# Token loads, attention bias rows, the gate store's queue and the place of four inverses, changed together in a two-layer hybrid backbone

## The chip, the cores and the metric

The kernel runs on one core of a Trainium2 chip. The metric is the device time of one execution in microseconds; where several runs were made, it is their median. The profile comes from one further execution.

## What is computed

A backbone of two layers over 256 latent tokens of 2048 features, with 256 context tokens. Layer 0 runs eight heads of a chunked, bidirectional gated DeltaNet beside eight heads of 2-D neighbourhood attention, all from one input projection; layer 1 is a gated short convolution. Each layer also has a SwiGLU feed-forward part of 5632 hidden features, and every normalised input is shifted and scaled by a modulation vector that is itself a product with a weight matrix. Cut to what matters here:

```python
sh1, sc1, g1, sh2, sc2, g2 = jnp.split(jax.nn.silu(c) @ ada_w[l] + ada_b[l], 6, axis=-1)
h = rmsnorm(x_lat, norm_mix[l]) * (1 + sc1) + sh1            # the same for the context tokens, with c_ctx
# gated DeltaNet: per 64-token chunk a triangular inverse, then a scan over the chunks
t_inv = lax.linalg.triangular_solve(eye + m, eye, left_side=True, lower=True, unit_diagonal=True)
# neighbourhood attention: bias by relative position, inside a band of columns only
s_loc = jnp.einsum('brqhd,brjkhd->bhrqjk', qg, kg) * scale + bias[None]
s_loc = jnp.where(in_win[:, None, :], s_loc, -jnp.inf)
# the DeltaNet output is normalised and gated, then both kinds of heads go through one projection
y_gdn = rmsnorm(o, g_norm) * jax.nn.silu(heads(z))
y = jnp.concatenate([y_gdn, y_na], axis=-1) @ w_out
```

## The kernel before

All matrices are float32. Every large product is made as three matmuls: a weight block of 128 x 1024 values is loaded (tile `raw`, L229), ScalarE rounds it to a high part (`whi`, L172), VectorE takes the rest (`wlo`, L243), and TensorE adds high times high, high times low and low times high. `fm_stream` (L306) leaves the result by features, `tm_stream` (L274) by tokens; each step of such a stream is one block of 128 input features. Four `raw` tiles are in flight, so the loads run a few steps ahead of TensorE.

The start. `start_block` (L524) loads 4 MB of the modulation weights in eight pieces (`araw0`, L530) and multiplies them by the conditioning vector (L533); `token_stats` (L565) loads the 512 tokens (`xn`, L569), squares them on ScalarE (L573), and scales them by their inverse norm on VectorE (L576). `start_tokens` (L537) turns one block's product into shift and scale (L540 to L552), transposes the scaled tokens, modulates them on ScalarE (L560, tile `modt`) and casts the result to `h` (L561, L562). The first stream, for the keys, takes up each block of `h` as it comes. Eight such blocks follow one another.

The middle. The projections for the attention queries, keys and values (`QB`, `KB`, `VB`) run as counted steps: 32 for the two halves of the queries, then 16 each for a half of the keys, a half of the values, and the same again. Beside them stands the gated DeltaNet. A list `plan` (L1127) says after which counted step its four pieces are queued, by the numbers in `P_INV`: the first inverse of the context, the second one with the matrices of the latent chunks and the context scans, the first inverse of the latent chunks, and the second one with the latent scores and scans (`first_inverse`, `second_inverse`, `latents`). `inverses` (L939) puts a 64-token inverse together from 32 x 32 blocks: small matmuls (L962, L969, L975), a copy with a minus sign on VectorE (L977) and one on ScalarE (L979). Its blocks come back from a scratch array by sixteen small loads on SyncE (L936). The rest of the modulation, `ada_mixer` (L366), is summed on VectorE (`acc`, L389) from loads on SyncE (`araw`, L384) and closed on TensorE (L396); it runs beside all of this.

The end of the mixer. `na_scores` (L1172) loads one head's bias rows in two halves into `br`, adds the band mask on VectorE into `bq` (L1183), makes the scores (L1187, L1188) and the softmax; `na_values` (L1200) makes the outputs. `za_evac` (L1215) makes the DeltaNet's gate with Silu from the last projection and stores it to the scratch array `zd`; `latent_out` reads it back after the scans. Then the output projection (`ev_w_out`) runs as a stream, in the order of the input groups 2, 0, 1, 3: two groups of attention heads around the two of DeltaNet heads.

Each engine works through its own queue in order, and so do the queues of the DMA issues. A scheduler at build time sets the order within each queue from a model of the engines, so an edit also moves instructions that it doesn't name. SyncE issues nearly all loads and stores; a wait in its queue holds back everything behind it.

Of the kernel before, what the change touches and what calls it, by code (L numbers as in the profile page):

```python
# [23 lines left out]
F32 = mybir.dt.float32  # L24
F32R = mybir.dt.float32r
AF = mybir.ActivationFunctionType
OP = mybir.AluOpType
# [12 lines left out]
GH = 6  # L40
YO = (2, 0, 1, 3)
NPT = 1
P_INV = (30, 32, 79, 80)
AB = 6
AHEAD = 6
LAG = 3
# [62 lines left out]
def body(tc, x, c, ctx, c_ctx, ada_w, ada_b, norm_mix, norm_ffn, ffn_w_gate, ffn_w_up, ffn_w_down,  # L109
# [3 lines left out]
    PE, ACT, DVE, POOL, SP = nc.tensor, nc.scalar, nc.vector, nc.gpsimd, nc.sync  # L113
# [410 lines left out]
    def start_block(b):  # L524

        pr = smt()
        for g in range(0, KT, 4):
            raw = sp.tile([128, 4, 2, 256], F32, name="araw0", tag="araw0", bufs=4)
            for s in range(2):
                SP.dma_start(raw[:, :, s, :], adr[:, g:g + 4, s, b * 256:(b + 1) * 256])  # L530
            for j in range(4):

                PE.matmul(pr[32 * j:32 * j + 32, :], cT2[:, g + j, :], raw[:, j].rearrange("p s n -> p (s n)"),  # L533
                          start=g == 0, stop=g == KT - 4)
        return pr
# [62 lines left out]
    zd = dram.tile([128, 2, 1024], F32, name="zd")  # L598
# [96 lines left out]
    def qa_evac(q):  # L695
# [11 lines left out]
                SP.dma_start(qTd[:, q * 4 + g * 2:q * 4 + g * 2 + 2, :], qf)  # L707
        return head_evac(2, q, 16, done, True)

    sums = start_block(0)  # L710
    token_stats()
    ka = [ka_evac(q) for q in range(2)]
    s0 = fm_stream([(wv, C_KA, 512)], ks, [0, 1], ka[0])
    s1 = fm_stream([(wv, C_KA + 512, 256)], ks, [0, 1], ka[1], gdt)
# [37 lines left out]
    for w in range(2):  # L752
        o = pw[:, w * 256:(w + 1) * 256]
# [407 lines left out]
    nap = pool("na", stack=nastk)  # L1161
# [3 lines left out]
    bandf = C("band")  # L1165
# [6 lines left out]
    def na_scores(h):  # L1172
        kb = nap.tile([128, 512], F32, name="kb", tag="kb", bufs=2)
        qb = nap.tile([128, 256], F32, name="qb", tag="qb", bufs=2)
        bq = nap.tile([128, 6, 64], F32, name="bq", tag="bq", bufs=2)
        br = nap.tile([128, 6, 64], F32, name="br", tag="br", bufs=1)
        for half in range(2):
            src = bass.AP(tensor=ev_rpb.tensor, offset=ev_rpb.offset + h * 465 + (5 - half) * 31 + 15 - 63,
                          ap=[[1, 64], [31, 6], [1, 64]])
            SP.dma_start(br[half * 64:half * 64 + 64], src)  # L1180
        SP.dma_start(kb, kb_d[:, h, :])
        SP.dma_start(qb, qb_d[:, h, :])
        DVE.tensor_tensor(bq, br, bandf[:, None, :].to_broadcast([128, 6, 64]), op=OP.add)  # L1183
        out_ = []
        for t in range(2):
            p = nat(h)
            PE.matmul(p, qb[:, t * 128:(t + 1) * 128], kb, start=True, stop=False)  # L1187
            PE.matmul(p[:, 0:256], C("flip"), bq[:, 2 - 2 * t:6 - 2 * t, :].rearrange("p s c -> p (s c)"),  # L1188
                      start=False, stop=True)
            s = nap.tile([128, 512], F32, name="s", tag="s", bufs=4)  # L1190
            m = nap.tile([128, 1], F32, name="m", tag="m", bufs=4)
            DVE.tensor_reduce(m, p, axis=AX.X, op=OP.max, negate=True)
            l = nap.tile([128, 1], F32, name="l", tag="l", bufs=4)
            ACT.activation(s, p, AF.Exp, bias=m, accum_out=l)
            DVE.reciprocal(l, l)
            DVE.tensor_scalar(s, s, l, None, op0=OP.mult)
            out_.append(s)
        return out_
# [16 lines left out]
    def za_evac(ti, n, p):  # L1215
        o = nsp.tile([128, 512], F32, name="zst", tag="nst", bufs=NST)
        ACT.activation(o, p, AF.Silu)
        ov = o.rearrange("p (h e) -> p h e", h=4)
        DVE.tensor_tensor(ov, ov, gnb[:, None, :].to_broadcast([128, 4, 128]), op=OP.mult)
        SP.dma_start(zd[:, ti, n * 512:(n + 1) * 512], o)  # L1220

    held = na_scores(0)
    for h in range(8):
# [279 lines left out]
```

## Time and profile before

| | |
|---|---|
| median of 3 runs | 2819.64 us (2818.58 to 2827.38) |
| the profiled execution | 2823.79 us |
| its span | 2822.0 us |
| mean granted TensorE clock | 0.989 |
| busy: TensorE, VectorE, ScalarE, GpSimd | 2719.8, 1920.1, 1301.9, 50.3 us |
| moved by DMA | 680.78 MB |

A row of the timeline has the start in us, the length in us, the engine, the line in the code, the operation, out<-in and how many instructions were merged; in brackets stands the idle time of the engine just before it and what ended it. SPq is SyncE's queue of DMA issues: its length is the issue, not the transfer. PE is TensorE, ACT ScalarE, DVE VectorE, POOL GpSimd. A row of the windows has the stretch, its length, and for each engine the busy time with the number of instructions, then the granted clock of TensorE, the share of time in which the DMA engines were busy, and GB/s.

### The profile page before, as it was taken

How to read it: one execution, taken by the hardware profiler on the slowest of the kernel's cores; microseconds unless marked ns; L12 is line 12 of the kernel's file. 1: busy time of each engine (PE TensorE's matmuls, PEld its weight loads, DVE VectorE, ACT ScalarE, POOL GpSimd, SP SyncE). 2: the span in 40 equal slices, each digit the busy share in tenths (PEclk: the TensorE clock that was granted, in tenths of full speed). 3: DMA queues.
4: the chain of work that ended last, by engine and by line, in shares of the span. 5: the costliest groups of instructions: out<-in, count | busy, mean ns of one | idle time of the engine just before them, and what ended most of it. 6: DMA issues, size and time to landing. Idle time of an engine off the chain costs nothing.

```text
span 2822.0 us, 40405 instructions
## 1 busy us (share of the span) xinstructions
PE 2719.8 (96%) x15113; PEld 2277.5 (81%) x15113; DVE 1920.1 (68%) x2647; ACT 1301.9 (46%) x1943; POOL 50.3 (2%) x77
## 2 busy tenths in 40 slices
PE   5999989999999999999999999999999999999998
PEld 3799989887778788888888878878878888888886
DVE  2377768866767888776678667797678644445665
ACT  2267534322454544444455555444454444444554
POOL 0000100000000000000000000000000000000000
PEclk9999999999999999999999999999999999999999
DMA  9945578887758699987788647998559766656663
GB/s 342 325 135 157 148 234 259 270 250 226 213 200 285 208 333 340 345 291 255 264 283 286 197 154 275 333 327 286 186 196 326 247 193 186 187 188 215 190 192 126
DMA packets 286399, 680.78 MB, mean 241 GB/s; under 512 B 57209, under 2 KB 100833, under 8 KB 284795
## 3 DMA queue, kind: packets, MB, share of 16 engines
q1 hardware_dynamic: 281828, 668.73, 71.3%
q10 hardware_dynamic: 4375, 9.48, 0.9%
q8 instruction: 118, 1.93, 0.3%
q14 instruction: 78, 0.64, 0.1%
HBM read 657.63 MB, written 20.48 MB: 240 GB/s over the span
## 4 chain that ended last, share of the span: by engine, by line
PE 78%; DMA 10%; DVE 6%; ACT 3%; issue 2%; SPq 1%; DVEq 0%; POOL 0%; ACTq 0%
PE mm L294 19%; PE mm L291 19%; PE mm L292 19%; PE mm L321 7%; DMA araw<-in_ada_w_dram 5%; PE mm L300 2%; PE mm L301 2%; PE mm L302 2%; DVE wlo L243 2%; PE sm L191 2%; DMA raw<-in_od_w_in_dram 1%; PE sm L533 1%; DVE acc L346 1%; DVE acc L389 1%; PE gd L321 1%
## 5 line engine op out<-in xcount | busy, mean ns | idle before, releaser
L243 DVE TENSOR_TENSOR wlo<-raw,whi 128x1024 fp32r<-128x1024 f32 x800 | 971.1, 1222 | 436.8 <-ACT whi L172 430.9
L172 ACT ACTIVATE whi<-raw 128x1024 fp32r<-128x1024 f32 x800 | 842.2, 1059 | 825.6 <-PE mm L294 618.9
L292 PE MATMUL mm<-wlo,fhi 128*128 128x512 f32 x1232 | 472.4, 392 | 0.0
L291 PE MATMUL mm<-whi,fhi 128*128 128x512 f32 x1232 | 470.7, 396 | 0.0
L294 PE MATMUL mm<-whi,flo 128*128 128x512 f32 x1232 | 392.2, 392 | 0.1
L346 DVE SCALAR_TENSOR_TENSOR acc<-araw,cT,acc 128x1024 f32<-128x1024 f32 x224 | 287.3, 1283 | 130.2 <-DMA araw<-in_ada_w_dram 123.5
L294 PEld LDWEIGHTS mm<-whi,flo 128*128 128x128 f32 x1232 | 230.8, 188 | 51.1 <-DVE flo L1288 0.5
L292 PEld LDWEIGHTS mm<-wlo,fhi 128*128 128x128 f32 x1232 | 231.8, 188 | 48.7
L291 PEld LDWEIGHTS mm<-whi,fhi 128*128 128x128 f32 x1232 | 231.9, 188 | 48.2
L291 PE MATMUL mm<-whi,ahi 128*128 128x512 f32 x672 | 259.8, 392 | 0.0
L292 PE MATMUL mm<-wlo,ahi 128*128 128x512 f32 x672 | 259.3, 391 | 0.0
L294 PE MATMUL mm<-whi,alo 128*128 128x512 f32 x672 | 209.8, 392 | 0.0
L321 PE MATMUL mm<-hllo,whi 128*128 128x256 f32 x608 | 172.9, 289 | 0.0
L321 PE MATMUL mm<-hlhi,whi 128*128 128x256 f32 x570 | 161.7, 292 | 2.2 <-DVE hlhi L561 1.9
L175 ACT ACTIVATE ahi<-prodT 128x256 fp32r<-128x256 f32 x176 | 73.2, 417 | 194.6 <-PE mm L292 183.9
L389 DVE SCALAR_TENSOR_TENSOR acc<-araw,cT,acc 128x512 f32<-128x512 f32 x192 | 142.7, 747 | 29.1 <-DMA araw<-in_ada_w_dram 27.3
L321 PE MATMUL mm<-hlhi,wlo 128*128 128x256 f32 x570 | 157.8, 289 | 0.0
L292 PEld LDWEIGHTS mm<-wlo,ahi 128*128 128x128 f32 x672 | 126.2, 188 | 27.7
L294 PEld LDWEIGHTS mm<-whi,alo 128*128 128x128 f32 x672 | 126.1, 188 | 27.3
L291 PEld LDWEIGHTS mm<-whi,ahi 128*128 128x128 f32 x672 | 126.2, 188 | 27.1
L292 PE MATMUL mm<-wlo,dhi 128*128 128x512 f32 x336 | 126.4, 396 | 2.2 <-DVE wlo L243 2.2
L291 PE MATMUL mm<-whi,dhi 128*128 128x512 f32 x336 | 123.8, 397 | 0.6 <-DVE u_t L1428 0.6
(419 smaller groups left out, 4194.0 us busy)
## 6 DMA issues: line engine op xcount, KB each, us to landing
araw<-in_ada_w_dram SPq DMA_DIRECT2D x288, 512.0 KB
raw<-in_ffn_w_down_dram SPq DMA_DIRECT2D x176, 512.0 KB
raw<-in_ffn_w_gate_dram SPq DMA_DIRECT2D x160, 512.0 KB
raw<-in_ffn_w_up_dram SPq DMA_DIRECT2D x160, 512.0 KB
raw<-in_ev_w_in_dram SPq DMA_DIRECT2D x112, 512.0 KB
araw<-in_ada_w_dram SPq DMA_DIRECT2D x192, 256.0 KB
raw<-in_od_w_in_dram SPq DMA_DIRECT2D x96, 512.0 KB
raw<-in_ev_w_out_dram SPq DMA_DIRECT2D x32, 512.0 KB
```

Source lines behind the costliest of these rows:

```text
L172: ACT.activation(dst, src, AF.Copy)
L175: ACT.activation(hi, src, AF.Copy)
L191: return PE.transpose(dst, src, ident[:n, :n])
L243: last_lo[0] = DVE.tensor_tensor(lo, raw, hi, op=OP.subtract).ins
L291: PE.matmul(ps[ti][n], a, hi[:, n * 512:(n + 1) * 512], start=first, stop=False)
L292: PE.matmul(ps[ti][n], a, lo[:, n * 512:(n + 1) * 512], start=False, stop=False)
L294: last_mm[0] = PE.matmul(ps[ti][n], b, hi[:, n * 512:(n + 1) * 512], start=False, stop=False).ins
L300: PE.matmul(ps[ti][n], lh(t), hi[:, c_], start=False, stop=False)
L301: PE.matmul(ps[ti][n], lh(t), lo[:, c_], start=False, stop=False)
L321: last_mm[0] = PE.matmul(ps[f][:, n * 256:(n + 1) * 256], wt, mv(w, k), start=False, stop=i == len(ks) - 1 and g == len(group) - 1 and j = ...
L346: DVE.scalar_tensor_tensor(acc, raw, cT[:, k:k + 1], acc, op0=OP.mult, op1=OP.add)
L389: DVE.scalar_tensor_tensor(accs[n], raws.pop(i), cT[:, k:k + 1], accs[n], op0=OP.mult, op1=OP.add)
```

## The change

There are four edits. The tokens' loads and statistics come ahead of the first block of modulation weights. The bias rows are loaded straight into `bq`, which gets a third buffer, and the mask is added in place; the tile `br` is gone. The gate's store to `zd` is issued by GpSimd instead of SyncE. The four pieces of the DeltaNet are queued two counted steps later each.

```diff
--- before.py
+++ after.py
@@ -40,7 +40,7 @@
 GH = 6
 YO = (2, 0, 1, 3)
 NPT = 1
-P_INV = (30, 32, 79, 80)
+P_INV = (32, 34, 81, 82)
 AB = 6
 AHEAD = 6
 LAG = 3
@@ -707,8 +707,8 @@
                 SP.dma_start(qTd[:, q * 4 + g * 2:q * 4 + g * 2 + 2, :], qf)
         return head_evac(2, q, 16, done, True)
 
+    token_stats()
     sums = start_block(0)
-    token_stats()
     ka = [ka_evac(q) for q in range(2)]
     s0 = fm_stream([(wv, C_KA, 512)], ks, [0, 1], ka[0])
     s1 = fm_stream([(wv, C_KA + 512, 256)], ks, [0, 1], ka[1], gdt)
@@ -1172,15 +1172,14 @@
     def na_scores(h):
         kb = nap.tile([128, 512], F32, name="kb", tag="kb", bufs=2)
         qb = nap.tile([128, 256], F32, name="qb", tag="qb", bufs=2)
-        bq = nap.tile([128, 6, 64], F32, name="bq", tag="bq", bufs=2)
-        br = nap.tile([128, 6, 64], F32, name="br", tag="br", bufs=1)
+        bq = nap.tile([128, 6, 64], F32, name="bq", tag="bq", bufs=3)
         for half in range(2):
             src = bass.AP(tensor=ev_rpb.tensor, offset=ev_rpb.offset + h * 465 + (5 - half) * 31 + 15 - 63,
                           ap=[[1, 64], [31, 6], [1, 64]])
-            SP.dma_start(br[half * 64:half * 64 + 64], src)
+            SP.dma_start(bq[half * 64:half * 64 + 64], src)
         SP.dma_start(kb, kb_d[:, h, :])
         SP.dma_start(qb, qb_d[:, h, :])
-        DVE.tensor_tensor(bq, br, bandf[:, None, :].to_broadcast([128, 6, 64]), op=OP.add)
+        DVE.tensor_tensor(bq, bq, bandf[:, None, :].to_broadcast([128, 6, 64]), op=OP.add)
         out_ = []
         for t in range(2):
             p = nat(h)
@@ -1217,7 +1216,7 @@
         ACT.activation(o, p, AF.Silu)
         ov = o.rearrange("p (h e) -> p h e", h=4)
         DVE.tensor_tensor(ov, ov, gnb[:, None, :].to_broadcast([128, 4, 128]), op=OP.mult)
-        SP.dma_start(zd[:, ti, n * 512:(n + 1) * 512], o)
+        POOL.dma_start(zd[:, ti, n * 512:(n + 1) * 512], o)
 
     held = na_scores(0)
     for h in range(8):
```

From L1176 on a line's number is one lower in the changed code. What the scheduler makes of the change, at three places. First SyncE at the start of the program; `araw` is a block's modulation weights (two loads a row), `xn` the tokens, `raw` the stream's weights. Before:

```order
L493 DMA cs<-in_cst_dram 128x128
L530 DMA araw_144<-in_ada_w_dram 128x4x256 x2
L530 DMA araw_151<-in_ada_w_dram 128x4x256 x2
L530 DMA araw_158<-in_ada_w_dram 128x4x256 x2
L530 DMA araw_165<-in_ada_w_dram 128x4x256 x2
L569 DMA xn<-in_x_dram 128x2048 x2
L569 DMA xn<-in_ctx_dram 128x2048 x2
L530 DMA araw_241<-in_ada_w_dram 128x4x256 x2
L229 DMA raw<-in_ev_w_in_dram 128x2x512
```

and now:

```order
L493 DMA cs<-in_cst_dram 128x128
L569 DMA xn<-in_x_dram 128x2048 x2
L569 DMA xn<-in_ctx_dram 128x2048 x2
L530 DMA araw_176<-in_ada_w_dram 128x4x256 x2
L530 DMA araw_183<-in_ada_w_dram 128x4x256 x2
L530 DMA araw_190<-in_ada_w_dram 128x4x256 x2
L530 DMA araw_197<-in_ada_w_dram 128x4x256 x2
L229 DMA raw<-in_ev_w_in_dram 128x2x512
```

The four loads of tokens moved from behind the first block's eight weight loads to their front, and the first stream weights stand ahead of the second block's loads.

Then TensorE at the first inverse. `hlhi` and `hllo` are the two parts of the latent tokens, `hclo` is the context's, `xd` and `n` are the inverse's blocks, `acc` the mixer's modulation. Before, its small matmuls followed one another, with 24 stream matmuls of the query projection still behind them:

```order
L321 MATMUL mm<-hllo,whi 128x256
L321 MATMUL mm<-hlhi,wlo 128x256
L962 MATMUL gd<-xd,n_3970 32x32 x32
L396 MATMUL sm<-cs,acc 128x1 x4
L969 MATMUL gd<-xdT,Y 32x32 x32
L975 MATMUL gd<-Y,xdT 32x32 x32
L321 MATMUL mm<-hlhi,whi 128x256
L321 MATMUL mm<-hllo,whi 128x256
```

Now the inverse begins after those 24, at the boundary to the key projection (L317 is its first matmul, `h_100` the first feature block of the tokens), and the sums of `acc` stand ahead of the 24:

```order
L321 MATMUL mm<-hlhi,wlo 128x256 x2
L321 MATMUL mm<-hlhi,whi 128x256
L321 MATMUL mm<-hllo,whi 128x256
L321 MATMUL mm<-hlhi,wlo 128x256
L962 MATMUL gd<-xd,n_3970 32x32 x32
L317 MATMUL mm<-h_100,whi 128x512
L321 MATMUL mm<-hllo,whi 128x256
L321 MATMUL mm<-hclo,whi 128x256
L321 MATMUL mm<-h_100,wlo 128x256 x2
```

The inverse's second group, L969, now stands behind 22 matmuls of the key projection instead of right behind the first. The third inverse moved in the same way, from 48 matmuls ahead of the boundary between the second keys and the second values to 38 matmuls (of 512 columns) behind it.

Last, SyncE around the first weights of the output projection (`ev_w_out`). Before, the gate's stores (`zd`) stand among them:

```order
L384 DMA araw<-in_ada_w_dram 128x512 x2
L1220 DMA zd<-zst 128x512 x2
L1202 DMA vb<-vb_d 128x4x128
L1220 DMA zd<-zst 128x512
L229 DMA raw<-in_ev_w_out_dram 128x1024 x2
L1181 DMA kb<-kb_d 128x512
L1182 DMA qb<-qb_d 128x256
L229 DMA raw<-in_ev_w_out_dram 128x1024
```

and now:

```order
L384 DMA araw<-in_ada_w_dram 128x512 x2
L229 DMA raw<-in_ev_w_out_dram 128x1024 x6
L1201 DMA vb<-vb_d 128x4x128
L229 DMA raw<-in_ev_w_out_dram 128x1024
L384 DMA araw<-in_ada_w_dram 128x512
L229 DMA raw<-in_ev_w_out_dram 128x1024
```

The stores left for GpSimd's queue; the loads of the attention heads stand elsewhere among the weights. On ScalarE the same stretch, where `zst` is the gate, `s` and `PT` belong to the attention, `yhi` is an output, and `o_t` and `vn` belong to the scans. Before:

```order
L1217 ACT_TABLE_LOAD
L1217 ACTIVATE zst<-mm 128x512 x2
L175 ACTIVATE yhi<-sm 128x256
L1194 ACT_TABLE_LOAD
L1194 ACTIVATE s,l<-sm,m 128x512
L1217 ACT_TABLE_LOAD
L1217 ACTIVATE zst<-mm 128x512
L1038 ACTIVATE vn<-gd,beta 128x128 x4
L1217 ACTIVATE zst<-mm 128x512
```

and now:

```order
L1193 ACTIVATE s,l<-sm,m 128x512
L1216 ACT_TABLE_LOAD
L1216 ACTIVATE zst<-mm 128x512 x4
L1016 ACTIVATE o_t<-gd,eg 128x128 x4
L172 ACTIVATE whi<-raw 128x1024
L175 ACTIVATE yhi<-sm 128x256
L172 ACTIVATE whi<-raw 128x1024
L1024 ACTIVATE vd<-gd,brest 128x128 x4
```

The four gates follow one another, with one load of the Silu table ahead of them instead of two.

## The prediction

> **What bounds the kernel now.** I read the page first (span, busy time, chain), then the windows, then the timeline of each engine at the four places where the code changes.
>
> ```profile
> span 2822.0 us, 40405 instructions
> PE 2719.8 (96%) x15113; PEld 2277.5 (81%) x15113; DVE 1920.1 (68%) x2647; ACT 1301.9 (46%) x1943; POOL 50.3 (2%) x77
> PE 78%; DMA 10%; DVE 6%; ACT 3%; issue 2%; SPq 1%; DVEq 0%; POOL 0%; ACTq 0%
> ```
>
> TensorE is busy for 2719.8 of 2822.0 us, so at most 102 us can be won without taking work away, and the change takes none away: it only moves waits. The order of the instructions is the same from the later part of the output projection on, so the whole effect lies before that. In the next two windows (us; then PE busy, its instructions, the other engines, PEclk, DMA share, GB/s) TensorE is full: 0.114 us for a 256-column matmul of the stream, 0.227 us for a 512-column one.
>
> ```profile
> 580.00:590.00 10.00, 10.00 (x88) 10.00 (x87) 5.75 (x10) 2.57 (x6) 1.81 (x1) 1.00 0.84 172
> 890.00:900.00 10.00, 10.00 (x44) 8.07 (x43) 9.81 (x11) 4.10 (x4) 0.00 (x0) 1.00 0.95 332
> ```
>
> **Part 1, tokens ahead of the modulation weights.** Timeline of the start:
>
> ```profile
> 14.96 0.82 SPq L569 DMA_DIRECT2D xn<-in_x_dram  x2
> 21.26 1.94 PE L533 MATMUL sm<-araw,cT 128*32 128x512 f32 x8 [1.15 <-DMA araw<-in_ada_w_dram]
> 26.17 0.16 DVE L552 TENSOR_TENSOR sc<-sc,vecT 128x4 f32<-128x4 f32 x1
> 30.99 1.91 ACT L573 ACTIVATE junk<-xn 128x2048 f32<-128x2048 f32 x1 [0.51 <-DMA xn<-in_ctx_dram]
> 35.30 1.06 ACT L172 ACTIVATE whi<-raw 128x1024 fp32r<-128x1024 f32 x1 [0.79 <-DMA raw<-in_ev_w_in_dram]
> 35.34 4.87 DVE L576 TENSOR_SCALAR xn<-xn,n0r 128x2048 f32<-128x2048 f32 x4
> 40.78 1.93 ACT L560 ACTIVATE modt<-sm,sh,sc 128x256 f32<-128x256 f32 x4 [1.59 <-PE sm L191]
> 45.43 2.08 PE L317 MATMUL mm<-h,whi 128*128 128x512 f32 x4
> ```
>
> Shift and scale are ready at 26.33, but the last tokens land only at 30.99, and their squares, the root and the four scalings (4.87) then stand bare until the first modulated tile at 40.78; the stream starts at 45.43, 4.65 later. With the tokens first, that statistics work lies beside the weight loads, and the weights land last, at about 31 (the same bytes in the same queue). From the last L533 to a ready scale it is 26.33 - 21.26 = 5.1, so 31 + 5.1 + 4.65 = 40.7 at the latest; the first weight of the stream, too, has the two loads of the next block (1 MB) no longer ahead of it. Gain 4.7, and up to 6.5 if the 8 KB rows of the tokens load faster than the weights' 1 KB rows. Does it survive? The load is near its limit until 140:
>
> ```profile
> 100.00:120.00 20.00, 20.00 (x168) 16.48 (x167) 7.62 (x21) 5.75 (x9) 0.00 (x0) 1.00 1.00 320
> 120.00:140.00 20.00, 20.00 (x168) 14.35 (x166) 8.48 (x20) 5.00 (x9) 0.00 (x0) 1.00 1.05 333
> 140.00:160.00 20.00, 20.00 (x169) 18.58 (x162) 8.43 (x19) 7.33 (x12) 0.00 (x0) 1.00 0.44 144
> 142.34 0.99 PE sm L533 x8
> ```
>
> The DMA share falls only after 140, and the last weights of this stage are used at 142.34. TensorE is full here, so it is the bound, but by little: a TensorE that runs 5 us ahead would want those bytes at 137. I take -4.5, with ends -6.5 and 0. That cover is what the term rests on.
>
> **Part 2, bias rows straight into their tile.** The DMA and the add stay, the intermediate tile with one buffer goes, so head 1's and head 2's rows no longer wait for the add of the head before.
>
> ```profile
> 687.34 1.13 PE L838 MATMUL gd<-cs,gm 128*128 128x128 f32 x8 [0.50 <-DVE gm L834]
> 696.13 0.56 DVE L1183 TENSOR_TENSOR bq<-br,cs 128x384 f32<-128x384 f32 x1 [5.74 <-DMA br<-in_ev_rpb_dram]
> 697.88 0.50 PE L292 MATMUL mm<-wlo,hlhi 128*128 128x512 f32 x1 [2.27 <-DVE wlo L243]
> 701.60 2.08 PE L838 MATMUL gd<-cs,gm 128*128 128x128 f32 x8 [2.99 <-DVE AT L1074]
> 705.93 0.56 DVE L1183 TENSOR_TENSOR bq<-br,cs 128x384 f32<-128x384 f32 x1 [3.79 <-DMA br<-in_ev_rpb_dram]
> 700.00:710.00 10.00, 8.40 (x27) 6.13 (x28) 6.21 (x13) 2.98 (x6) 0.00 (x0) 0.68 0.65 167
> ```
>
> VectorE takes its queue in order: for 5.74 us it waits for the rows, and the weight split and the mask product behind it keep TensorE waiting 2.27 and 2.99. After that TensorE runs at 0.68 of its clock: 8.40 us of work that at full clock is 5.7, so 2.7 more, and the same eight L838 take 2.08 instead of 1.13. Together 8.0. The Trainium skill (TensorE: Matmul & The Clock Gate, Part 1) has the clock fall only after an idle window of about 3.4 us; by that neither wait would slow it and the term would be at most 5.3, but the 0.68 stands in the row, so the trace decides. In the new order head 1's rows are asked for right behind head 0's, yet still on the same busy queue, so some of the wait may stay: I take -5, ends -8 and 0.
>
> **Part 3, gate store from GpSimd.** SyncE's queue and what hangs on it:
>
> ```profile
> 764.05 0.57 SPq L1202 DMA_DIRECT2D vb<-vb_d  x1
> 768.79 0.69 DVE L1219 TENSOR_TENSOR zst<-zst,gnb 128x512 f32<-128x512 f32 x1 [1.22 <-ACT zst L1217]
> 769.51 0.32 SPq L1220 DMA_DIRECT2D zd<-zst  x1
> 769.88 0.92 SPq L229 DMA_DIRECT2D raw<-in_ev_w_out_dram  x2
> 776.41 1.20 PE L291 MATMUL mm<-whi,yhi 128*128 128x512 f32 x4 [3.01 <-ACT whi L172]
> 388.37 7.68 DMA qb_d<-nst
> ```
>
> SyncE stands from 764.6 to 769.5 behind a store whose tile VectorE has not finished, and the first weights of the output projection are issued only then; TensorE waits 3.01 for them. Moved to GpSimd's idle queue the store holds nobody. But the new order of ScalarE puts the four gates one behind the other, and with two tiles the third has to wait until the first store has landed, with VectorE's next scan step behind it. No row shows a store from GpSimd; the nearest is one of the same kind of tile from SyncE, 7.68 us. Covered, the term is -3.0; bare, the wait is 7.68 instead of 3.01, +4.7. I take -1.5, since the loads of the stream, which sat ahead of that store in its own queue, aren't ahead of this one. The Trainium skill's fit for a GpSimd DMA (DMA: Bandwidth & Descriptors, Anatomy of one DMA) would make it 2.6 us, an estimate; by it the term is -3.0.
>
> **Part 4, inverses two steps later.**
>
> ```profile
> 415.20 2.21 SPq L229 DMA_DIRECT2D raw<-in_ev_w_in_dram  x4
> 415.26 0.75 PE L962 MATMUL gd<-xd,n 32*32 32x32 f32 x64
> 415.98 1.02 PE L396 MATMUL sm<-cs,acc 128*128 128x1 f32 x8
> 420.81 1.06 ACT L172 ACTIVATE whi<-raw 128x1024 fp32r<-128x1024 f32 x1 [4.37 <-DMA raw<-in_ev_w_in_dram]
> 421.08 0.48 PE L975 MATMUL gd<-Y,xdT 32*32 32x32 f32 x18 [2.98 <-issue]
> 421.92 0.58 PE L321 MATMUL mm<-hlhi,whi 128*128 128x256 f32 x1 [0.36 <-ACT whi L172]
> 420.00:430.00 10.00, 8.56 (x88) 8.13 (x88) 7.98 (x11) 7.18 (x13) 0.00 (x0) 0.67 0.87 275
> 616.29 0.44 PE L962 MATMUL gd<-xd,n 64*64 64x64 f32 x2 [4.13 <-DVE xd L977]
> ```
>
> The weights that TensorE needs after 415.26 are issued at 415.20, behind the inverse's own loads, and land at 420.81. So the 6.66 us to 421.92 are a wait for weights, of which TensorE uses 6.66 - 2.98 - 0.36 = 3.3, about 0.9 of it for the mixer's sums (L396), which stay where they are, and 2.4 for the first inverse. In the new order the inverse stands behind the two steps that wait for those weights, and its 2.4 us come later: +2.4. The third inverse waited 4.13 for a copy on VectorE; 14.3 us later in the stream (48 matmuls of 0.114 before the boundary of two streams, now 38 of 0.227 behind it, 5.5 + 8.6) the copy should be due in time: -4.1 to 0, I take -2. The latent scans start later, too, and at their end more of them may stand bare. A step there is 4.99 us long:
>
> ```profile
> 810.92 1.06 PE L1000 MATMUL gd<-state,kT 128*128 128x128 f32 x8
> 815.91 1.06 PE L1000 MATMUL gd<-state,kT 128*128 128x128 f32 x8
> ```
>
> TensorE works for most of such a step, so one more costs a part of it: +1.6, ends 0 and 5. Part 4 together: +2, ends -4 and +7.
>
> **The sum.** -4.5 - 5 - 1.5 + 2 = -9.0. The profiled execution took 2823.79 (span 2822.0 and 1.8 around it), 4.2 above the median of 2819.64, so I make the sum against it, 2814.8, and take the same 9.0 off the median: 2810.6, given as 2811.
>
> **The rivals.** *The same bytes on the same engines.* Parts 1 and 3 only reorder transfers. If the loads until 140 are what TensorE really follows, and the output weights land no earlier, both are worth nothing: -5 + 2 = -3, 2817. For it: the DMA shares of 1.00 and 1.05. Against it: TensorE full there, and SyncE's 4.9 us stand. The Trainium skill says the like (DMA: Bandwidth & Descriptors, Issuing engines are not separate DMA queues): another issuer saves only the sequencer's time; that would be the 0.32 us of the store's row, while the trace has the wait. *Every wait goes* (the lower ends): -6.5 - 8 - 3 - 4 = -21.5, 2798. For it: each wait has one releaser which the change moves; against it: some of the covers compete for one DMA queue. *Slower: the latent chain becomes the bound.* From the third inverse to the last scan each step hangs on the one before. If the 14.3 us by which it is queued later aren't made up, group 0 of the output projection comes 14.3 later, and the waits of parts 2 and 3, which lie beside that chain, give nothing: 14.3 - 4.5 = +9.8, 2829. It decides as soon as TensorE has no stream matmul left while scans remain, as between 810.92 and 815.91, where the order has none; against it: a step has four or more groups of eight matmuls like the rows above, so most of its 4.99 us is TensorE's own work, which costs the same wherever it stands. *The change doesn't do what it says*: the rows of the orders show that it does, 0.
>
> **How the numbers follow.** A measurement of this kernel can tell about 0.3%, 8.5 us, from no change: 2811.2 is the line. Forecast 0.45 (2805 to 2817: 0.27 below the line, 0.18 above), same bytes 0.20, every wait goes 0.20, slower 0.15. Faster 0.27 + 0.20 = 0.47, within 0.18 + 0.20 = 0.38, slower 0.15. The range takes in the lower ends at 2798 and leaves out most of the slower case: 2798 to 2826.
>
> **What would show it.** Right: the first L317 near 40 and no new wait for araw before 140; no VectorE wait over 2 us for head 1's and head 2's rows, and a clock of 1.00 where the 0.68 stands; the output weights issued before the last gate. Wrong: TensorE waiting for L533's data between 60 and 140; ScalarE waiting for a GpSimd store; a wait of over 5 us ahead of the first inverse's weights; the last scan more than 10 us behind the last stream matmul of the first half's group 2.

## The result, and the profile after

The changed kernel takes 2837.75 us (median of 6 runs, 2834.55 to 2840.86), the kernel before 2825.08 beside it (6 runs, 2818.58 to 2828.2). The ratio is 1.0048, with a 95% interval of 1.0035 to 1.0060: some 12.7 us slower, where 9 us faster was forecast. The profiled execution of the changed kernel took 2834.55 us, the fastest of its six, with a span of 2832.8, 10.8 more than the one before.

The head of its page:

```profile
span 2832.8 us, 40395 instructions
PE 2726.1 (96%) x15113; PEld 2282.1 (81%) x15113; DVE 1920.6 (68%) x2647; ACT 1297.7 (46%) x1940; POOL 58.2 (2%) x81
```

The number of TensorE's instructions is the same, and its busy time rose by 6.3 us: waiting, and work at a lower clock, not more work. The last transposition of the softmax weights into `sm` (L191) starts at 834.23 before and at 846.42 after, 12.2 later; the two spans differ by 10.8, so nothing is added behind it. The loss is ahead of that point, as the prediction had said that the whole effect would be.

**Start (part 1).** TensorE's timeline: the first matmul of the stream, and the last group of the modulation.

```profile
38.52 2.07 PE L317 MATMUL mm<-h,whi 128*128 128x512 f32 x4 [0.57 <-DVE h L561]
149.61 0.95 PE L546 MATMUL sm<-cs,mrow 128*128 128x2 f32 x8
```

The stream starts 6.9 us earlier (38.52 against 45.43), and the last group of the modulation starts 3.1 later (149.61 against 146.48 before), behind as many matmuls as before (850 and 851). In two windows of that stretch (us; PE busy, then the other engines, PEclk, DMA share, GB/s) TensorE's clock is lower:

```profile
60.00:80.00 20.00, 18.93 (x134) 12.63 (x134) 5.91 (x14) 4.04 (x6) 0.00 (x0) 0.91 1.09 353
100.00:120.00 20.00, 18.50 (x138) 12.94 (x137) 6.51 (x15) 4.04 (x6) 0.00 (x0) 0.91 0.90 291
```

Before, the first of them was no fuller, but at full clock:

```profile
60.00:80.00 20.00, 18.51 (x146) 12.69 (x146) 7.73 (x21) 4.80 (x8) 0.00 (x0) 1.00 1.05 335
```

The second was full and had 168 matmuls in the prediction's row, against 138 here. SyncE's waits between 0 and 160 show who holds the loads: SyncE waits for TensorE to free the buffers of `araw` (us in total, times, longest).

```profile
SPq L530 <- PE sm L533: 30.0, 17, 4.1
```

Before, that was 16.8 us in 12 waits. The modulation matmuls stand in TensorE's order between matmuls of the stream, which now starts sooner.

**Bias rows (part 2).** Two of VectorE's eight bias additions (start, us, engine and line, tile, idle time before and its releaser):

```profile
694.73 0.56 DVE L1182 TENSOR_TENSOR bq<-bq,cs 128x384 f32<-128x384 f32 x1 [1.71 <-DMA bq<-in_ev_rpb_dram]
758.31 0.56 DVE L1182 TENSOR_TENSOR bq<-bq,cs 128x384 f32<-128x384 f32 x1 [4.64 <-DMA bq<-in_ev_rpb_dram]
```

The first of them is head 2's. The 5.74 and 3.79 us of heads 1 and 2 are down to 1.57 and 1.71. But all eight additions now wait for their rows, 19.2 us together, where four waited 14.6. SyncE issues the rows of the later heads about as late as before, and the addition stands sooner behind them: the rows for the addition at 758.31 are issued at 749.87; before, those for the one at 770.45 were issued at 752.39.

**Gate store (part 3).** ScalarE's third Silu; then VectorE's first multiplication, GpSimd's first store, the chain's piece for its transfer, and TensorE behind all that:

```profile
769.93 0.60 ACT L1216 ACTIVATE zst<-mm 128x512 f32<-128x512 f32 x1 [13.12 <-DMA zd<-zst]
```

```profile
759.82 0.68 DVE L1218 TENSOR_TENSOR zst<-zst,gnb 128x512 f32<-128x512 f32 x1
760.81 0.68 POOL L1219 DMA_DIRECT2D zd<-zst  x1 [89.34 <-DVE zst L1218]
760.81 9.01 DMA zd<-zst
772.35 2.08 PE L1020 MATMUL gd<-R,xdT 128*128 128x128 f32 x8 [7.01 <-DVE R L1003]
```

The first gate is through Silu at 754.86. VectorE, in order, waits until 758.31 for bias rows, so it multiplies the gate at 759.82, GpSimd issues the store at 760.81, and it lands 9.01 later. Until then the third Silu has no tile: 13.12 us of ScalarE, and 7.01 of TensorE, since VectorE's `R` stands behind the third gate. This is the bare end of part 3, made longer by part 2.

**Inverses (part 4).** TensorE at the wait for weights near 415, the first inverse, the first scan, the last stream matmul of group 2 and the last scan:

```profile
423.26 0.58 PE L321 MATMUL mm<-hlhi,whi 128*128 128x256 f32 x1 [7.87 <-ACT whi L172]
428.65 0.75 PE L962 MATMUL gd<-xd,n 32*32 32x32 f32 x64
524.48 1.05 PE L1020 MATMUL gd<-vtok,xdT 128*128 128x128 f32 x8
801.07 0.63 PE L294 MATMUL mm<-whi,ylo 128*128 128x512 f32 x2
830.44 1.16 PE L1020 MATMUL gd<-R,xdT 128*128 128x128 f32 x8 [0.24 <-DVE R L1003]
```

The wait is 7.87 us and empty. The scans start 19.3 later than before (505.17) and end 12.2 later (818.26). Between the last stream matmul and the last scan there are 29.4 us, before 20.4.

### The profile page after: what moved, and what is told of

It reads as the page before. It is cut to its first block, busy times and chain, and to the rows that moved or that the text cites. A ratio compares the mean times of both kernels' runs of the same rounds, so it can differ in the third digit from the quotient of the medians.

```text
span 2832.8 us, 40395 instructions
## 1 busy us (share of the span) xinstructions
PE 2726.1 (96%) x15113; PEld 2282.1 (81%) x15113; DVE 1920.6 (68%) x2647; ACT 1297.7 (46%) x1940; POOL 58.2 (2%) x81
## 3 DMA queue, kind: packets, MB, share of 16 engines
q0 software_dynamic: 320, 1.05, 0.1%
## 4 chain that ended last, share of the span: by engine, by line
PE 76%; DMA 11%; DVE 6%; ACT 3%; issue 3%; SPq 1%; DVEq 0%; POOL 0%; ACTq 0%
PE mm L291 17%; PE mm L294 17%; PE mm L292 17%; PE mm L321 10%; DMA araw<-in_ada_w_dram 6%; DVE wlo L243 2%; PE sm L191 2%; DVE acc L346 2%; PE mm L300 2%; PE mm L302 2%; PE mm L301 2%; DMA bq<-in_ev_rpb_dram 1%; PE sm L533 1%; PE gd L321 1%; ACT whi L172 1%
## 5 line engine op out<-in xcount | busy, mean ns | idle before, releaser
L321 PE MATMUL mm<-hlhi,whi 128*128 128x256 f32 x570 | 161.9, 292 | 10.8 <-ACT whi L172 7.9
```

What stands on the lines that cost most here:

```text
L321: last_mm[0] = PE.matmul(ps[f][:, n * 256:(n + 1) * 256], wt, mv(w, k), start=False, stop=i == len(ks) - 1 and g == len(group) - 1 and j = ...
```

## The experiments

Each kernel was timed against the kernel before on the same chip; the ratio is to those runs. In all, 18 further kernels ran. The four entries of `P_INV` are called the first pair (first inverse; second inverse with the scans behind it) and the last pair. My first theory, from the trace above, was **scans late**: the chain from the first inverse to the last scan starts 19 us late and ends the stretch. Its rivals were the gate store and the start.

### One part at a time on the kernel before

Tokens alone:

```diff
-    sums = start_block(0)
     token_stats()
+    sums = start_block(0)
```

> The kernel before with the tokens first and nothing else. Theory scans late (the two inverses, queued two steps later, start the delta-rule scans some 19 us later and these end the stretch): nothing of the loss is here; the kernel stays within 3 us of before, first L317 near 38.5 instead of 45.43, and whatever the start gains or loses is taken up by the time the scans begin. Theory gate store (the third Silu waits for the store that GpSimd issued, and the scans' work behind it on ScalarE is late): the same. Theory start (the transfers, not TensorE, are the bound up to 145 us, and the tokens first leave the DMA engines idle for part of the first 20 us): the last modulation row L546 is 3 us later than before and the kernel 2 to 4 us slower.

Measured: 2828.28 us, ratio 1.0015 (1.0002 to 1.0029). The last group of the modulation:

```profile
150.17 0.95 PE L546 MATMUL sm<-cs,mrow 128*128 128x2 f32 x8
```

The stream starts 6.9 us earlier, at 38.53, and the modulation ends 3.7 later. So part 1 doesn't gain 4.5; it loses about 4.

Bias rows alone:

```diff
-        bq = nap.tile([128, 6, 64], F32, name="bq", tag="bq", bufs=2)
-        br = nap.tile([128, 6, 64], F32, name="br", tag="br", bufs=1)
+        bq = nap.tile([128, 6, 64], F32, name="bq", tag="bq", bufs=3)
...
-        DVE.tensor_tensor(bq, br, bandf[:, None, :].to_broadcast([128, 6, 64]), op=OP.add)
+        DVE.tensor_tensor(bq, bq, bandf[:, None, :].to_broadcast([128, 6, 64]), op=OP.add)
```

> The kernel before with the bias rows straight into their tile. All theories: within 3 us of before. Where the prediction's part 2 holds, 4 to 6 us faster with no VectorE wait over 2 us ahead of the bias addition; where the rows' transfer is issued as late as before, the wait of VectorE stays (14.6 us in all before) and so does the time.

Measured: 2824.5 us, ratio 0.9999 (0.9986 to 1.0013). What VectorE's additions waited for, in the view of the tile `bq`, and TensorE behind them:

```profile
  DMA bq<-in_ev_rpb_dram: 22.9, 8
```

```profile
696.27 2.08 PE L838 MATMUL gd<-cs,gm 128*128 128x128 f32 x8 [3.95 <-DVE AT L1074]
```

Eight waits of 22.9 us together, and TensorE's wait ahead of the eight L838 is 3.95 instead of 2.99, with the same slow 2.08 behind it. SyncE's issue of head 2's rows, before and here:

```profile
696.71 1.28 SPq L1180 DMA_DIRECT2D br<-in_ev_rpb_dram  x2
```

```profile
681.24 2.12 SPq L1179 DMA_DIRECT2D bq<-in_ev_rpb_dram  x2
```

Before, the addition at 696.13 ends at 696.69, and the rows go out 0.02 later: the tile `br` had kept them late, as the prediction said. Without it they go out 15.5 us sooner, and heads 1 and 2 wait 2.28 and 2.34 instead of 5.74 and 3.79. But the last five additions, which waited 0.81 together before, now wait 13.7, up to 5.10 for one.

Gate store alone:

```diff
-        SP.dma_start(zd[:, ti, n * 512:(n + 1) * 512], o)
+        POOL.dma_start(zd[:, ti, n * 512:(n + 1) * 512], o)
```

> The kernel before with the gate store issued by GpSimd. Theory gate store: ScalarE waits 8 us or more for the third Silu, TensorE for R behind it, and the kernel is 6 to 12 us slower, 2831 to 2837. Theory scans late: the scans are 19 us earlier here than in the kernel after, so such a wait finds slack, and the kernel is within 3 us of before.

Measured: 2821.43 us, ratio 0.9988 (0.9975 to 1.0002). The third Silu:

```profile
773.01 0.60 ACT L1217 ACTIVATE zst<-mm 128x512 f32<-128x512 f32 x1
```

It waits for no store here; the second stands at 764.94, and some 8 us lie between them, with other work of ScalarE. Theory gate store falls as the cause of the whole loss.

Inverses alone:

```diff
-P_INV = (30, 32, 79, 80)
+P_INV = (32, 34, 81, 82)
```

> The kernel before with the inverses two steps later and nothing else. Theory scans late: first L1020 near 524 instead of 505, last ScalarE vn (L1038) some 12 us after 819.5, and the kernel 9 to 14 us slower, 2834 to 2839. Theory gate store: within 3 us of before, since the scans' ScalarE work waits for no store here.

Measured: 2839.81 us, ratio 1.0049 (1.0030 to 1.0069), with the first L1020 at 523.43. The whole loss is in this one line. The reverse, the kernel after with the old entries:

```diff
-P_INV = (32, 34, 81, 82)
+P_INV = (30, 32, 79, 80)
```

> The kernel after with the four inverse entries as before; tokens first, bias rows direct and the gate store by GpSimd stay. Theory scans late: nearly the whole loss is gone, 2820 to 2828, last L1020 near 820. Theory gate store (the 13.1 us wait of the third Silu costs by itself): still 2831 to 2837.

Measured: 2825.59 us, ratio 1.0006 (0.9996 to 1.0016). That the four entries cost the time is shown from both sides.

### Which entries

First pair late, last pair late and all four entries two steps earlier, in this order:

```diff
-P_INV = (30, 32, 79, 80)
+P_INV = (32, 34, 79, 80)
+P_INV = (30, 32, 81, 82)
+P_INV = (28, 30, 77, 78)
```

> The kernel before with only the first two of the four inverse entries two steps later (32, 34, 79, 80). Theory one chain (the scans run back to back from the first inverse on, so their late start of some 18 us is carried to the end): 2832 to 2838, 9 to 14 us slower, first L1020 near 523 and last L1020 near 830. Theory last pair (between the halves there is slack that takes up the late start, and only the queueing of the last inverses sets the end): within 4 us of before, last L1020 within 4 us of 818.26.

> The kernel before with only the last two inverse entries two steps later (30, 32, 81, 82). Theory one chain: within 4 us of before, since the chain starts as early as before. Theory last pair: 2832 to 2838, 9 to 14 us slower, last matmul of the inverses (L962) near 663 instead of 641 and last L1020 near 830.

> The kernel before with all four inverse entries two steps earlier (28, 30, 77, 78). If the scans end the stretch already in the kernel before (a latent bound in both kernels): 2812 to 2818, 6 to 12 us faster, last L1020 10 us earlier than 818.26. If in the kernel before the scans just keep up with the stream: within 4 us of before. If the stream needs the later place of the inverses to fill its own waits: slower by up to 5 us.

Measured: the first pair late 2839.22 us, ratio 1.0054 (1.0042 to 1.0066); the last pair late 2822.07, ratio 0.9995 (0.9985 to 1.0006); all four earlier 2810.55, ratio 0.9951 (0.9936 to 0.9967). At this point all three agreed with one chain of scans that starts late. One row spoke against it. These are the last stream matmul of group 2 and the last scan with the last pair late:

```profile
782.97 1.27 PE L294 MATMUL mm<-whi,ylo 128*128 128x512 f32 x4
817.30 1.16 PE L1020 MATMUL gd<-R,xdT 128*128 128x128 f32 x8 [0.25 <-DVE R L1003]
```

The scans end 34.3 us behind the stream, more than in the kernel after (29.4), and the kernel loses nothing: the stream had only come earlier (782.97 against 797.83 before). A long bare tail isn't a loss by itself.

So the second entry was moved alone, by two steps and by six, which leaves the first inverse in the wait near 415 and makes the scans late all the same; and the two halves of the earlier entries were tried, and four steps. In the order of the texts that follow:

```diff
-P_INV = (30, 32, 79, 80)
+P_INV = (30, 34, 79, 80)
+P_INV = (30, 36, 79, 80)
+P_INV = (30, 32, 77, 78)
+P_INV = (28, 30, 79, 80)
+P_INV = (26, 28, 75, 76)
```

> The kernel before with the second entry alone two steps later (30, 34, 79, 80). The first inverse then still stands in the wait for weights near 415; the first scan matmul (L1020) stands 60 matmuls into the value stream instead of 38, where the first pair late put it at 103. Theory scans late (the loss goes with the scans' place): 22 matmuls of 65, a third of the 15 us, 2827 to 2832. Theory uncovered wait (the loss of the first pair is the 7.5 us wait for weights near 415 that the first inverse no longer fills, and the slow clock behind it): within 3 us of before.

> The kernel before with the second entry alone six steps later (30, 36, 79, 80). The first inverse still stands in the wait near 415; the first scan matmul stands 125 matmuls into the value stream and the last quads' first score matmul (L1009) 531 into the output projection, against 103 and 534 with the first pair late, 38 and 484 before. Theory late scans: as slow as the first pair late or slower, 2835 to 2845. Theory uncovered wait: within 4 us of before, 2820 to 2828. In between: both, by the share.

Measured: 2825.44 us, ratio 1.0008 (0.9998 to 1.0018), and 2825.57 us, ratio 1.0001 (0.9989 to 1.0012). First scan and last scan, with the first pair late:

```profile
525.70 1.05 PE L1020 MATMUL gd<-vtok,xdT 128*128 128x128 f32 x8
834.31 1.16 PE L1020 MATMUL gd<-R,xdT 128*128 128x128 f32 x8 [0.24 <-DVE R L1003]
```

and with the second entry very late:

```profile
525.69 1.05 PE L1020 MATMUL gd<-vtok,xdT 128*128 128x128 f32 x8
822.66 1.16 PE L1020 MATMUL gd<-R,xdT 128*128 128x128 f32 x8 [0.24 <-DVE R L1003]
```

The scans start at the same time in both, 20.5 later than before, and the one kernel is 15 us slower than before while the other isn't slower. **Theory scans late has fallen.** The plainest pair is (30, 34) and (32, 34), with the same last pair: they differ in the first entry alone and have 1.0008 and 1.0054. The first inverse's place makes the difference, not when the scans start.

> The kernel before with only the last two entries two steps earlier (30, 32, 77, 78). Theory that the gain of the four earlier entries is the last pair's (last inverse matmul L962 8.2 us earlier there, while the first L1020 moved only 0.9): 2808 to 2815. Theory that it is the first pair's (one chain from the first scan on): within 4 us of before.

> The kernel before with only the first pair two steps earlier (28, 30, 79, 80). If the parts add up, the four earlier entries (13.5 us faster) less the last pair earlier (4 us faster) leave 9 us: 2812 to 2818. If the gain needs both pairs: within 4 us of before.

> The kernel before with all four entries four steps earlier (26, 28, 75, 76). If the gain goes on with the steps (6.8 us each from two steps later to two earlier): 2796 to 2803. If two steps already reach what the order can give, since the scans cannot start before the last of the value projection's data: within 4 us of the four entries two steps earlier, 2807 to 2815. If the inverses now stand ahead of their own data (the triangular solve, the loads of the diagonal blocks): slower than that.

Measured: last pair earlier 2820.07 us, ratio 0.9986 (0.9975 to 0.9997); first pair earlier 2820.26, ratio 0.9987 (0.9978 to 0.9996); all four steps earlier 2825.18, ratio 0.9995 (0.9981 to 1.0009). Some 4 us each, 13.5 together, and nothing for four steps: the gain doesn't go on with the steps. By the medians it doesn't add up by parts either, but there the intervals nearly meet: by the ratios the parts sum to 7.6 us, 4 either way, and all four together gain 13.8, 4.4 either way.

### The wait near 415 itself

The weights that end this wait are issued behind sixteen small loads of the inverses' diagonal blocks (L936) on SyncE. To take the wait away, these loads were given to GpSimd, with the inverses as before and with the first pair late:

```diff
-    def load_diag(dz, q):
+    def load_diag(dz, q, by=SP):
...
-                SP.dma_start(m_, dz[v, b, q].rearrange("d t (r c) -> r (d t) c", r=32))
+                by.dma_start(m_, dz[v, b, q].rearrange("d t (r c) -> r (d t) c", r=32))
...
-    diag = [load_diag(parts[2], q) for q in range(2)]
+    diag = [load_diag(parts[2], q, POOL) for q in range(2)]
```

> The kernel before with the sixteen loads of the first inverses' diagonal blocks (L936) issued by GpSimd in place of SyncE, so that the weights behind them are issued some 10 us earlier. Both theories: the wait for weights near 415 (whi, some 6.7 us, that the first inverse partly fills) goes or falls below 2 us, and the kernel is 0 to 6 us faster, 2818 to 2824; if GpSimd's loads land late, TensorE waits for xd ahead of the first inverse instead and the kernel is 0 to 5 us slower.

> The same with the first pair two steps later (32, 34, 79, 80). Theory uncovered wait: with no wait for weights left to fill, the later first pair costs next to nothing against the run with the loads on GpSimd alone, within 4 us of it. Theory scans late: 9 to 15 us slower than that run, as it was against the kernel before, with the added waits of TensorE spread between 550 and 850.

Measured: 2851.49 us, ratio 1.0094 (1.0080 to 1.0107), and 2853.11 us, ratio 1.0104 (1.0091 to 1.0118). With the inverses as before, the first and the last of the sixteen loads on GpSimd, and TensorE ahead of the first inverse:

```profile
401.21 0.77 POOL L936 DMA_DIRECT2D xdT<-dz  x1 [1.38 <-DMA dz<-lsol]
455.07 0.65 POOL L936 DMA_DIRECT2D xd<-dz  x1 [2.63 <-issue]
438.79 0.28 PE L962 MATMUL gd<-xd,n 32*32 32x32 f32 x2 [16.71 <-issue]
```

GpSimd takes 54 us for what SyncE issues in 10 (402.3 to 412.7 before), and TensorE waits 16.71 us. The wait for weights went, but a larger one took its place in both kernels, and the pair can't tell the theories apart. It failed as a control.

### The gate store and the bias rows together

The kernel after with the store on SyncE again, and two versions on the kernel before with the four earlier entries: with bias rows and store, and with the store alone.

```diff
-        POOL.dma_start(zd[:, ti, n * 512:(n + 1) * 512], o)
+        SP.dma_start(zd[:, ti, n * 512:(n + 1) * 512], o)
```

> The kernel after with the gate store issued by SyncE again, all else as after. Theory that the 13.1 us wait of the third Silu (7.0 us of it on TensorE, for R) costs by itself: 2830 to 2834, 4 to 8 us faster than the kernel after. Theory that the wait lies where the late scans leave room: within 3 us of the kernel after, 2835 to 2841.

> The kernel before with the four inverses two steps earlier (28, 30, 77, 78), the bias rows direct and the gate store by GpSimd, the tokens not moved: 2803 to 2811, at or a little below the four earlier entries alone (2810.6), since the store alone gave 2 us and the bias rows nothing. If the parts disturb each other: 2811 to 2820.

> The kernel before with the four inverses two steps earlier and the gate store by GpSimd, the bias rows through br as before. Theory bias and store together (VectorE, in order, waits for bias rows ahead of the gate's multiplication, so the store starts late and the third Silu waits for it): no Silu wait over 5 us here, and 2806 to 2813 as with the earlier inverses alone. Theory that the store alone takes the gain back: a Silu wait of 10 us and 2818 to 2826.

Measured: the kernel after with SyncE's store 2833.32 us, ratio 1.0038 (1.0024 to 1.0053), against 1.0048 for the kernel after; the intervals overlap, so what the store costs in the kernel after lies between nothing and some 8 us and isn't settled. Earlier entries with both edits 2822.83, ratio 1.0000 (0.9991 to 1.0009); with the store alone 2811.53, ratio 0.9950 (0.9936 to 0.9964). The first of these two lies above both ranges that were expected. The bias rows, which cost nothing alone, cost 11 us here by the medians. (The two traces that follow differ by 6.5 us only: 2818.45, the fastest of its eleven, and 2811.97.) With both, VectorE and ScalarE show the pattern of the kernel after:

```profile
758.30 0.56 DVE L1182 TENSOR_TENSOR bq<-bq,cs 128x384 f32<-128x384 f32 x1 [5.35 <-DMA bq<-in_ev_rpb_dram]
758.78 0.68 DVE L1218 TENSOR_TENSOR zst<-zst,gnb 128x512 f32<-128x512 f32 x1
```

```profile
766.51 0.60 ACT L1216 ACTIVATE zst<-mm 128x512 f32<-128x512 f32 x1 [10.85 <-DMA zd<-zst]
```

With the store alone:

```profile
753.90 0.69 DVE L1219 TENSOR_TENSOR zst<-zst,gnb 128x512 f32<-128x512 f32 x1 [1.22 <-ACT zst L1217]
```

```profile
762.41 1.24 ACT L1217 ACTIVATE zst<-mm 128x512 f32<-128x512 f32 x2 [6.67 <-DMA zd<-zst]
```

VectorE multiplies the first gate right behind its Silu, and the third Silu's wait falls from 10.85 to 6.67; I had expected less than 5. TensorE's longest wait between 740 and 800 is 1.73 us then, against 3.39. That the two edits disturb each other is shown by the times; that the whole 11 us go this way isn't, since those waits of TensorE differ by less.

## Why the prediction was wrong

The step that failed is part 4: +2, with ends −4 and +7. It measured about +14 (inverses alone, 1.0049; 1.0030 to 1.0069 is 8 to 19 us). Its sum priced the waits of two inverses and the end of the scans; what the new order makes of the waits between the first scan and the last transposition had no term, and in three traces with the first pair late it is 8 to 10 us there (3 in a fourth). Beside it, the covers of parts 1 and 2 failed. Parts 1 to 3, forecast at −11, came to +4, 0 and −3 alone, and to some +2 together (the kernel after with the old entries, 1.0006; 0.9996 to 1.0016). So the miss of some 22 us is about as much theirs (13) as part 4's (12).

**Part 1, −4.5: the cover failed.** The text rested on "TensorE is full here, so it is the bound". The DMA share of 1.00 and 1.05 in the same rows was the better sign. The start gained 6.9 us, more than the 4.7 to 6.5 that were given. By the last group of the modulation that had become a loss of 3.1. TensorE's own waits between 40 and 160 grew only from 3.3 to 3.8 us, and none is for the weights of L533, so the sign that was set for this case didn't show. New are two stretches of 3.4 us at half clock (from 73.6 and 107.7 on), and SyncE waited 30.0 us instead of 16.8 for buffers that only TensorE frees. Which of these took the 10 us back isn't shown. The rival of the same bytes, which put this part at nothing, was nearer.

**Part 2, −5: right for heads 1 and 2, and the wait moved.** `br`'s one buffer did hold their rows, and the waits of 5.74 and 3.79 shrank. But the later heads' additions came to stand right behind their rows, and VectorE waited more in all (22.9 us against 14.6, bias rows alone). The text had kept "some of the wait may stay"; it had no term for the later heads. The slow L838 of 2.08 us came back behind one wait of 3.95 (bias rows alone); in the kernel after the same eight take 1.13 behind a shorter one:

```profile
696.69 1.13 PE L838 MATMUL gd<-cs,gm 128*128 128x128 f32 x8 [1.96 <-DVE gm L834]
```

But the clock falls there too, only later: it is 0.50 from 698.2 to 701.6, and the two score matmuls (L1186) at 698.62 take 2.07 us instead of the 1.02 of their like at 688.33. The Trainium skill's idle window of some 3.4 us (TensorE: Matmul & The Clock Gate, Part 1) agrees with the wait of 3.95; the 2.27 and 2.99 of before, 0.73 apart, and the 1.96 here it doesn't explain if each wait counts alone.

**Part 3, −1.5: not contradicted alone** (0.9988, some 3 us; the interval, 0.9975 to 1.0002, holds both the forecast and zero), and the bare end came true only in company. The 9.01 of the store in the kernel after lies above the bound of 7.68 that was taken from SyncE's row. The Trainium skill's fit (DMA: Bandwidth & Descriptors, Anatomy of one DMA) had 2.6 as an estimate; the four stores of the kernel after took 2.3 to 9.0, with a median of 5.4, so the measurement decides against the fit as a price under load.

**Part 4: terms for the wrong places.** The sum had the first inverse's work out of the wait near 415 (+2.4), the third inverse's wait (−2) and the end of the scans (+1.6). (By its own terms the lower end is 2.4 − 4.1 = −1.7 and not −4, and the 14.3 us, 5.5 + 8.6, are 14.1.) The last pair late, 0.9995, shows nothing of the third inverse. Near 415 the loss can't be seen either. With the second entry very late the first inverse's first three groups are done by 416.8, and the wait ends at the same 423.26 as in the kernel after:

```profile
416.34 0.48 PE L975 MATMUL gd<-Y,xdT 32*32 32x32 f32 x18 [1.06 <-issue]
423.26 0.58 PE L321 MATMUL mm<-hlhi,whi 128*128 128x256 f32 x1 [6.45 <-ACT whi L172]
```

An empty wait as long as the kernel after's 7.87 stands there behind the first inverse in its old place, too: 7.30 in the kernel after with the old entries (1.0006) and 7.95 with the last pair earlier (0.9986), and neither kernel is slow.

What is lost by the first scan can be counted. In TensorE's order 38 matmuls of the value stream stand ahead of it before, 103 with the first pair late, 125 with the second entry very late; at 0.227 us each, 20.5 us of lateness hold 14.8 and 19.7 us of stream work. That leaves 5.8 and 0.8 us lost, in the kernel after, where it is 103 too, 4.6 (19.3 less 14.8, in rounded numbers), and with the inverses alone 3.5. But single traces don't tell such amounts apart: the bias rows alone, the last pair late, the kernel before and the gate store alone have the same order on TensorE, VectorE, ScalarE and SyncE up to 500, and their first scan starts at 503.26, 503.89, 505.17 and 510.67. With the four entries earlier (first scan at 504.24, 18 matmuls ahead of it) 3.6 us are lost there as well, and what those entries gain falls behind it.

More is lost between the first scan and the last transposition. These are the windows between these two events in four kernels, before, first pair late, second entry very late, four entries earlier (length; PE busy; ...; PEclk third from the end; the traced execution of the four entries earlier is the slowest of its six, 2817.28):

```profile
505.17:834.23 329.06, 306.80 (x2240) 262.66 (x2239) 231.12 (x446) 123.91 (x266) 9.22 (x11) 0.97 0.73 231
```

```profile
525.70:850.29 324.59, 297.86 (x2175) 254.94 (x2174) 219.15 (x432) 123.00 (x263) 10.11 (x11) 0.96 0.70 221
```

```profile
525.69:837.87 312.18, 286.43 (x2153) 244.74 (x2152) 216.75 (x428) 122.75 (x264) 9.31 (x12) 0.99 0.71 229
```

```profile
504.24:826.77 322.53, 307.38 (x2262) 263.68 (x2261) 231.53 (x449) 123.75 (x268) 11.13 (x14) 0.99 0.74 240
```

Idle time is length less busy. The slow clock takes half of TensorE's busy time in the stretches that the trace shows at a clock of 0.50 (before: 614.3 to 621.2, 699.7 to 706.5 and from 829.4 on):

| kernel | idle | slow clock | sum | against before |
|---|---|---|---|---|
| before | 22.3 | 6.7 | 28.9 | |
| first pair late | 26.7 | 11.8 | 38.5 | +9.6 |
| second entry very late | 25.8 | 4.3 | 30.1 | +1.2 |
| four entries earlier | 15.2 | 3.2 | 18.4 | −10.5 |

The lengths of the windows, less the stream matmuls by which they differ (65, 87 and 20 at 0.227 us), say the like: +10.3, +2.9 and −11.1. By lengths it is +7.6 in the kernel after, +9.2 with the inverses alone, and +3.0 in the kernel after with SyncE's store, whose trace is the fastest of its six.

So the kernels differ here by TensorE's waits of 2 to 4 us and the slow clock behind them. TensorE's waits from 505 to 855 that are over 2.0 us, before (us in total, times, longest):

```profile
PE gd L962 <- DVE xd L977: 4.1, 1, 4.1
PE gd L1211 <- ACT PT L167: 3.7, 1, 3.7
PE mm L291 <- ACT whi L172: 3.0, 1, 3.0
PE gd L838 <- DVE AT L1074: 3.0, 1, 3.0
PE mm L292 <- DVE wlo L243: 2.3, 1, 2.3
```

with the four entries earlier:

```profile
PE gd L1211 <- ACT PT L167: 3.7, 1, 3.7
PE mm L292 <- DVE wlo L243: 2.8, 2, 2.1
```

and with the first pair late:

```profile
PE sm L1187 <- ACT s L1194: 4.1, 1, 4.1
PE gd L962 <- DMA xd<-dz: 3.9, 1, 3.9
PE gd L1211 <- ACT PT L167: 3.7, 1, 3.7
PE gd L1009 <- DMA qT<-qTd: 2.8, 1, 2.8
PE gd L1028 <- ACT vd L1024: 2.7, 1, 2.7
```

Earlier entries lose three waits of before (4.1, 3.0, 3.0) and half of the slow clock. Late ones trade them for others of the same size, for a load, a softmax or a scan step that now comes at a bad moment. No single wait is shown to be the cause.

**The slower rival** had the sign, at 2829 against 2837.75, but by a mechanism that fell. It let the latent chain become the bound, to decide "as soon as TensorE has no stream matmul left while scans remain". The last pair late meets that condition more than the kernel after (34.3 us against 29.4) and costs nothing. The sign that was set for it, the last scan more than 10 us behind the stream, was there in the kernel before (20.4).

**What stays open:** which property of the first inverse's place makes the waits behind the first scan worse, by 8 to 10 us in three traces and 3 in a fourth. That it isn't the start of the scans is shown; that it is the order that the scheduler makes around each wait is argued from the views only. Kernels that differ in one entry or one pair lie up to 15 us apart.

Two versions beat both kernels: the four entries two steps earlier (2810.55 us, ratio 0.9951, 0.9936 to 0.9967), with or without the gate store on GpSimd (2811.53, 0.9950). Both leave the tokens and the bias rows as they were.

## What to carry to other kernels

Before moving a piece of filler work, look at the waits that the new order makes behind it, and not only at the one that it filled: here the loss didn't show at that wait, and most of it lay where the sum had no term. A DMA share of 1.00 stood beside a full TensorE here, and the earlier start was given back: a full engine alone was no proof that it was the bound. Test edits alone and in company: one that does nothing alone (bias rows) took 11 us from a good order. And before reading a few us out of two traces, compare traces of kernels whose order is the same up to that point.

## What the runs showed of the hardware

Sixteen loads of small pieces (32 partitions, 16 by 32 elements) issued by GpSimd came 2 to 7 us apart, 401.21 to 455.72, where SyncE issued most of the same ones 0.5 us apart. GpSimd's store of a 256 KB tile landed after 2.3 to 9.0 us in one kernel and 6.2 to 7.4 in another. Four kernels with the same order up to 500 us reached the same matmul at times up to 7.4 us apart. And two traces with the scans' start at the same place differ by 7.5 us of slow clock behind TensorE's waits (11.8 against 4.3 us).
